# Queries and keys of a dilated attention layer: one wide matmul for both parts of the tokens, and the rotary swap as transfers

## The chip, the core and the metric

The kernel runs on one core of a Trainium2 chip. The metric is the device time of one execution in microseconds (us), the median of three runs. A profile of one more execution comes with it; its rows give the times of single instructions on the engines: TensorE (PE; its weight loads are PEld), VectorE (DVE), ScalarE (ACT), GpSimd (POOL), and SyncE (SP), which issues the loads of weights.

## What is computed

The reference is a trunk of two layers on 256 tokens of width 1024, in float32. The even layer mixes neighbourhood attention and latent attention, the odd layer is the one below, and a squared-ReLU MLP stands behind each.

```python
def odd_mixer(xn, w_in, w_o, cos_f, sin_f):
    hcat = (xn @ w_in).reshape(b, s, DIL_GROUPS, 3, DIL_HEADS, HEAD_DIM)
    q = apply_rope(hcat[:, :, :, 0], cos_f, sin_f)
    k = apply_rope(hcat[:, :, :, 1], cos_f, sin_f)
    v = hcat[:, :, :, 2]
    return dilated_attention(q, k, v) @ w_o

def apply_rope(x, cos, sin):
    x1, x2 = x[..., :half], x[..., half:]
    return jnp.concatenate([x1 * c - x2 * s, x2 * c + x1 * s], axis=-1)
```

There are 3 dilation groups of 16 heads with 64 columns each; `half` is 32. A product with float32 accuracy is made from float32r matmuls: tokens and weights are each split into a high and a low part, and high x high, low x high and high x low are summed.

## The kernel before

Activations lie transposed in SBUF, 8 tiles of 128 features by 256 tokens. `xh` and `xl` are the high and low part of the normed tokens, two tiles from one tag with two buffers. Weights stream in: SyncE loads 1 MB at a time into `raw`, ScalarE casts it to the high part `whi` (L201), VectorE subtracts to the low part `wlo` (L202), each in four pieces; a pool of three buffers holds them.

The function `odd` works in 8 units of two heads in each of three groups. In a unit, `qk_steps` makes three blocks (b = 0, 1, 2) of queries and keys. A block has two halves f of 128 output features and 256 tokens each, and for each half 8 tiles of input features are summed, so 16 calls of `mm3` (L204 to L207), each with three matmuls of 256 columns; both halves lie in one PSUM bank. `rope` (L928) then turns the block: ScalarE copies the four 32-partition quarters, swapped in pairs, from PSUM to the tile `sw` (L931, L932), VectorE multiplies the block by the cosine (L934) and `sw` by the sine (L935) and adds. Block 0 gives queries and keys of the first group (`q0h`, `q0l`), block 1 the queries of the other two (`q12`), block 2 their keys (`k12`, printed `k`, L944). `value_steps` makes the values. `attention` makes the scores of the unit before (L214 from block 0, L967 from `q12` and `k12`), the softmax (L974 to L978), and turned probabilities (L985); `mix` multiplies them with the values of the unit before that (L1000, L1005). `weave` lays these among the matmuls of the next unit.

The order on each engine is set by a scheduler at build time, from the order in which the program is written and its priorities; on the chip each engine takes its instructions in that order. PSUM banks come from two tags, `acc` and `w`, four each. All small temporaries (`sw`, `r1`, `sn`, `pp`) share the tag `scratch` with 12 buffers. GpSimd's queue carries transfers only in the two MLPs (L141, with accumulation).

Of the kernel before, what the change touches and what calls it, by code (L numbers as in the profile page):

```python
# [20 lines left out]
F32R = mybir.dt.float32r  # L21
# [28 lines left out]
def trunk(ctx, tc, a, out):  # L50
# [16 lines left out]

    def half_tile(pool, name, bufs, tag="half"):
        return pool.tile([P, KT, T], F32R, tag=tag, name=name, bufs=bufs)

    def quarter_pair(name):
        return [act.tile([P, KT // 2, T], F32R, tag="quarter", name=name + v, bufs=4) for v in "hl"]
# [119 lines left out]
    def weight():  # L192

        j = state["used"]
        prefetch(j + 1, j + 1)
        prefetch(j + LOAD_AHEAD, j + SPLIT_AHEAD)
        state["used"] = j + 1
        return parts.pop(j)[1:3]
# [38 lines left out]

    def prepare(k, n, xT, ts=slice(0, T)):

        v, hi, lo, gk = x[:, k, ts], xT[0][:, k, ts], xT[1][:, k, ts], gains[:, n * KT + k:n * KT + k + 1]  # L240
        return (lambda: nc.scalar.activation(hi, v, AF.Copy, scale=gk).ins,
                lambda: nc.vector.scalar_tensor_tensor(lo, v, gk, hi.bitcast(F32), ALU.mult, ALU.subtract).ins)  # L242

# [51 lines left out]

    def hand_over(accs, last, n):

        xT = half_tile(act, "xh", 2), half_tile(act, "xl", 2)
        s = sum_tile()
        for b in range(4):  # L300
            last[b]()
            v, acc = x[:, 2 * b:2 * b + 2, :], two(accs[b])
            with tc.high_priority(NORM_PRIO):
                nc.vector.tensor_tensor(v, acc, v, op=ALU.add)
                for f in zip(*(prepare(k, n, xT) for k in (2 * b, 2 * b + 1))):
                    done = [step() for step in f]

        with tc.issue_after(done[0]), tc.issue_after(done[1]):
            state["parts_done"] = [add_squares(b, s) for b in range(4)][-1]
        return xT, s  # L310
# [40 lines left out]
    def mlp(mp, xT, s, apart=(), beside=lambda j, p: None):  # L351

        hs = {}
        quarters = [act.tile([P, KT // 2, T], F32R, tag="quarter", name="hh", bufs=4) for _ in range(3)]

        def up(j, pu):
            w = weight()

            ranges = [range(4), range(4, 6), range(6, 8)] if j == 0 else [range(8)]
            for ks in ranges:
                for f in range(2):
                    for k in ks:
                        c = slice(k * 256 + f * P, k * 256 + f * P + P)
                        mm3(pu[:, (1 - f) * T:(2 - f) * T], w[0][:, c], w[1][:, c], xT[0][:, k, :], xT[1][:, k, :],
                            k == 0 and (f == 0 or j > 0), k == KT - 1 and (f == 1 or j > 0))
            r = scratch([512], "relu")
            nc.scalar.activation(r, pu, AF.Relu)
            h = mp.tile([P, 8, P], F32, tag="h", name="h", bufs=1)  # L370
            nc.scalar.activation(h[:, 4:8, :].rearrange("p (t f) n -> p f t n", f=2), r.rearrange("p (f t n) -> p f t n", f=2, t=2), AF.Square)
            hh = quarters[j % 3].rearrange("p a (b n) -> p (a b) n", n=P)
            hl = mp.tile([P, 7, P], F32R, tag="hl", name="hl", bufs=3)
            hs[j] = hh, hl
            if j < 14:
                nc.vector.tensor_tensor(h[:, 2:4, :], h[:, 7:8, :].broadcast_to([P, 2, P]), h[:, 5:7, :], op=ALU.subtract)
                nc.vector.tensor_tensor(h[:, 1, :], h[:, 5, :], h[:, 3, :], op=ALU.subtract)
                nc.vector.tensor_tensor(h[:, 0, :], h[:, 4, :], h[:, 1, :], op=ALU.subtract)  # L378
                split(hh[:, 0:7, :], hl, h[:, 0:7, :])
            else:  # L380
                split(hh[:, 0:4, :], hl[:, 0:4, :], h[:, 4:8, :])

        def down(j, m):
            wh, wl = weight()
            hh, hl = hs[j]
            first = j == 0
            for n, i, b in SEVEN:
                end = j == 13 and (n not in EIGHT or n in apart)
                mm3(m[n], hh[:, i, :], hl[:, i, :], wh[b], wl[b], first, end)
                if n == "Q3":  # L390
                    beside(j, m["C22"])

        for j in range(3):
            up(j, bank("w"))
        inv = inverse_columns(s)
        m = {n: bank("w" if n in ("P1", "P2", "Q6", "C22") else "acc") for n in ("P1", "P2", "Q6", "C22", "Q7", "Q5", "Q3", "Q4")}
        for j in range(14):
            if j:
                up(j + 2, m["C22"])
            down(j, m)  # L400
        tail = {j: weight() for j in (14, 15)}

        def last(n, o=None, c=slice(0, BLK)):
            o = m[n] if o is None else o
            new = n == "C22" or n in apart
            for j, w in tail.items():
                for i, (at, b) in enumerate(EIGHT[n]):
                    wh, wl = (z[:, b * BLK + c.start:b * BLK + c.stop] for z in w)
                    mm3(o, hs[j][0][:, at, :], hs[j][1][:, at, :], wh, wl, new and (j, i) == (14, 0), (j, i) == (15, 1))

        return m, last, inv
# [9 lines left out]
    def turn_over(m, last, inv, n):  # L421


        xT = half_tile(act, "xh", 2), half_tile(act, "xl", 2)
        s = sum_tile()
        i0, i1 = (column(inv, t) for t in range(NT))
        y = {}

        def turn(t, h, pt):
            with tc.high_priority(NORM_PRIO):  # L430
                for k in range(4):
                    nc.tensor.transpose(pt[:, k * P:(k + 1) * P], y[t, h][:, k * P:(k + 1) * P], ident)
                v = x[:, 4 * h:4 * h + 4, tok(t)]
                nc.vector.tensor_tensor(v, pt.rearrange("p (k n) -> p k n", k=4), v, op=ALU.add)
                for k in range(4 * h, 4 * h + 4):
                    done = [step() for step in prepare(k, n, xT, tok(t))]
            if (t, h) == (1, 0):
                with tc.issue_after(done[0]), tc.issue_after(done[1]):
                    for b in range(4):
                        add_squares(b, s)  # L440

        def step(o, name, scale, v, op=ALU.add):
            with tc.high_priority(NORM_PRIO):
                onto_tokens(o, m[name], scale, v, op)
            return o

        sc = lambda: scratch([512], "y")
        last("P2")
        p0, p1 = sc(), sc()
        nc.scalar.activation(p0, m["P1"], AF.Copy, scale=i0)  # L450
        nc.scalar.activation(p1, m["P1"], AF.Copy, scale=i1)
        y[0, 0] = step(sc(), "P2", i0, p0)
        v0 = step(sc(), "Q6", i0, p0, ALU.subtract)
        v0 = step(v0, "Q5", i0, v0)
        last("Q3")
        turn(0, 0, m["P1"])
        y[0, 1] = step(v0, "Q3", i0, v0)
        v1 = step(sc(), "Q6", i1, p1, ALU.subtract)
        v1 = step(v1, "Q7", i1, v1)
        v2 = step(sc(), "Q5", i1, v1)  # L460
        last("C22")
        turn(0, 1, m["Q6"])
        y[1, 1] = step(v2, "C22", i1, v2)
        last("Q4")
        y[1, 0] = step(v1, "Q4", i1, v1, ALU.subtract)
        return xT, s, [lambda: turn(1, 1, m["P2"]), lambda: turn(1, 0, m["P1"])]
# [81 lines left out]


    def even(ep):  # L550
        xT = xh, xl = half_tile(act, "xh", 2), half_tile(act, "xl", 2)

        def load_x(k, n):
            nc.sync.dma_start(x[:, k:k + n, :], a["x"][:, k:k + n, :])
# [308 lines left out]


    def odd(op, xT, s, late):
        xh, xl = xT
        cosT = op.tile([P, T], F32, name="cosT")
        sinT = op.tile([P, T], F32, name="sinT")
        mask = op.tile([P, NT, 384], F32, name="mask")
# [43 lines left out]
        def qk_steps(d):  # L913
# [3 lines left out]

            def gemm(b, f, half):
                if f == 0 and half == 0:
                    hold["w"], hold["p"] = weight(), bank("acc")  # L920
                (wh, wl), pq = hold["w"], hold["p"]
                for k in range(4 * half, 4 * half + 4):
                    ws = slice((f * KT + k) * P, (f * KT + k + 1) * P)
                    mm3(pq[:, f * T:(f + 1) * T], wh[:, ws], wl[:, ws], xh[:, k, :], xl[:, k, :], k == 0, k == KT - 1)
                if f == 1 and half == 1:
                    rope(b, pq)

            def rope(b, pq):  # L928
                sw, r1 = scratch([512], "sw"), scratch([2, T], "r1")
                for r in range(0, P, 64):  # L930
                    nc.scalar.copy(sw[r:r + 32], pq[r + 32:r + 64])  # L931
                    nc.scalar.copy(sw[r + 32:r + 64], pq[r:r + 32])  # L932
                sw = sw.rearrange("p (f n) -> p f n", f=2)
                nc.vector.tensor_tensor(r1, pq.rearrange("p (f n) -> p f n", f=2), cosT.unsqueeze(1).broadcast_to([P, 2, T]), op=ALU.mult)  # L934
                nc.vector.tensor_tensor(sw, sw, sinT.unsqueeze(1).broadcast_to([P, 2, T]), op=ALU.mult)  # L935
# [201 lines left out]
```

## Time and profile before

| | us |
|---|---|
| median of three runs | 737.83 |
| the runs | 737.17 to 737.85 |
| the profiled execution | 738.17 |
| its span | 736.4 |

The page gives each engine's busy time in the span: TensorE 727.2 us, VectorE 610.5, ScalarE 558.9, GpSimd 79.9. Its slices show the granted clock of TensorE at full speed but for the last. The odd layer lies between about 290 and 545 us. A time at the head of a row is a start, counted from the start of the span; matmuls overlap, so that their pace is read from the distance of two starts and not from their length.

### The profile page before, as it was taken

The page shows a single profiled execution, that of the slowest core. Times are in us where ns is not written, and L with a number is a line of the kernel's source. Part 1 is how long each engine was busy: PE and PEld are TensorE (multiplying, and loading weights), DVE is VectorE, ACT ScalarE, POOL GpSimd, SP SyncE. Part 2 cuts the span into 40 slices and gives each one's busy share as a digit, 9 for nine tenths or more (in the row PEclk, how much of TensorE's full clock was granted, in tenths as well). Part 3 has the DMA queues.
Part 4 walks back from the last instruction along what each step waited for, and adds up shares of the span by engine and source line. Part 5 has one row for each costly group of instructions (what it writes and reads, how often), then busy time and mean ns, then how long its engine had stood idle before and what let it go on. Part 6 is the DMA issues. An engine that isn't in the chain of part 4 may idle for free.

```text
span 736.4 us, 14008 instructions
## 1 busy us (share of the span) xinstructions
PE 727.2 (99%) x5442; PEld 680.7 (92%) x5442; DVE 610.5 (83%) x1090; ACT 558.9 (76%) x1027; POOL 79.9 (11%) x75
## 2 busy tenths in 40 slices
PE   9999999999999999999999999999999999999996
PEld 6988899999999998999999999999999999999995
DVE  6888859999999959887778677776759999999957
ACT  7778968767766756888988989889867768767752
POOL 0100002224212000000000000000003123322000
PEclk9999999999999999999999999999999999999998
DMA  8773338798999643644443444534558699898611
GB/s 312 275 263 131 115 115 216 227 288 236 263 266 261 194 145 150 226 146 140 173 160 144 156 151 171 176 129 160 199 204 216 208 275 262 247 263 249 190 52 57
DMA packets 34178, 143.78 MB, mean 195 GB/s; under 512 B 3776, under 2 KB 5312, under 8 KB 25024
## 3 DMA queue, kind: packets, MB, share of 16 engines
q1 hardware_dynamic: 26208, 127.94, 49.6%
q0 software_dynamic: 7616, 14.68, 12.0%
q8 instruction: 42, 0.69, 0.4%
q10 hardware_dynamic: 288, 0.28, 0.1%
q14 instruction: 24, 0.20, 0.1%
HBM read 141.84 MB, written 1.05 MB: 194 GB/s over the span
## 4 chain that ended last, share of the span: by engine, by line
PE 92%; DVE 4%; ACT 1%; issue 1%; DMA 1%; POOL 0%; SPq 0%; POOLq 0%; DVEq 0%
PE acc L205 17%; PE acc L206 16%; PE acc L207 16%; PE w L205 11%; PE w L206 11%; PE w L207 11%; PE w L214 1%; PE w L985 1%; DVE wlo L202 1%; PE w L801 1%; PE w L967 1%; PE acc L1000 1%; PE w L815 1%; ACT whi L201 1%; DVE xl L242 1%
## 5 line engine op out<-in xcount | busy, mean ns | idle before, releaser
L202 DVE TENSOR_TENSOR wlo<-raw,whi 128x512 fp32r<-128x512 f32 (+3 forms) x360 | 297.0, 846 | 56.0 <-ACT whi L201 55.6
L201 ACT CAST whi<-raw 128x512 fp32r<-128x512 f32 (+3 forms) x360 | 253.8, 745 | 89.4 <-PE w L206 64.8
L206 PE MATMUL w<-xl,whi 128*128 128x256 f32 x528 | 149.6, 283 | 0.1
L207 PE MATMUL w<-xh,wlo 128*128 128x256 f32 x528 | 149.3, 283 | 0.0
L205 PE MATMUL w<-xh,whi 128*128 128x256 f32 x528 | 148.9, 283 | 0.0
L205 PE MATMUL acc<-xh,whi 128*128 128x256 f32 x432 | 125.2, 290 | 0.0
L206 PE MATMUL acc<-xl,whi 128*128 128x256 f32 x432 | 122.3, 283 | 0.0
L207 PE MATMUL acc<-xh,wlo 128*128 128x256 f32 x432 | 122.3, 283 | 0.0
L206 PEld LDWEIGHTS w<-xl,whi 128*128 128x128 f32 x528 | 101.2, 192 | 1.6 <-DVE xl L242 0.6
L205 PEld LDWEIGHTS w<-xh,whi 128*128 128x128 f32 x528 | 101.0, 192 | 1.0
L207 PEld LDWEIGHTS w<-xh,wlo 128*128 128x128 f32 x528 | 101.2, 192 | 0.0
L140 POOL COPY sum<-sum 128x512 f32<-128x512 f32 x28 | 41.4, 1494 | 468.3 <-DVE wlo L202 271.9
L205 PEld LDWEIGHTS acc<-xh,whi 128*128 128x128 f32 x432 | 82.5, 191 | 1.3 <-issue 0.3
L206 PEld LDWEIGHTS acc<-xl,whi 128*128 128x128 f32 x432 | 82.5, 191 | 0.0
L207 PEld LDWEIGHTS acc<-xh,wlo 128*128 128x128 f32 x432 | 82.4, 191 | 0.0
L205 PE MATMUL acc<-whi,xh 128*128 128x384 f32 (+2 forms) x160 | 55.4, 348 | 0.2 <-ACT whi L201 0.2
L206 PE MATMUL acc<-wlo,xh 128*128 128x384 f32 (+2 forms) x160 | 55.1, 344 | 0.4 <-DVE wlo L202 0.4
L207 PE MATMUL acc<-whi,xl 128*128 128x384 f32 (+2 forms) x160 | 54.7, 342 | 0.0
L201 ACT CAST hh<-h 128x896 fp32r<-128x896 f32 (+1 forms) x32 | 28.9, 903 | 18.2 <-DVE h L378 17.2
L205 PE MATMUL w<-whi,hh 128*128 128x512 f32 (+1 forms) x108 | 42.1, 390 | 0.0
L206 PE MATMUL w<-wlo,hh 128*128 128x512 f32 (+1 forms) x108 | 41.5, 384 | 0.0
L207 PE MATMUL w<-whi,hl 128*128 128x512 f32 (+1 forms) x108 | 41.2, 382 | 0.0
(225 smaller groups left out, 1495.4 us busy)
## 6 DMA issues: line engine op xcount, KB each, us to landing
raw<-in_w SPq DMA_DIRECT2D x36, 1024.0 KB, 5.4
raw<-in_w_oqk SPq DMA_DIRECT2D x24, 1024.0 KB, 4.8
raw<-in_w SPq DMA_DIRECT2D x28, 768.0 KB, 5.3
sum<-in_w POOLq DMA_DIRECT2D x28, 512.0 KB, 8.5
raw<-in_w_ov SPq DMA_DIRECT2D x16, 768.0 KB, 4.3
sum<-in_w SPq DMA_DIRECT2D x28, 256.0 KB, 6.1
raw<-in_w_oe SPq DMA_DIRECT2D x4, 1024.0 KB, 6.6
raw<-in_w_oo SPq DMA_DIRECT2D x4, 1024.0 KB, 4.8
```

The source lines that it names most:

```text
L140: nc.gpsimd.tensor_copy(out=sums[:, 1, :], in_=sums[:, 0, :])
L201: a = nc.scalar.copy(hi, src).ins
L202: return a, (eng or nc.vector).tensor_tensor(lo, src, hi.bitcast(F32), op=ALU.subtract).ins
L205: nc.tensor.matmul(o, sh, mh, start=first, stop=False)
L206: nc.tensor.matmul(o, sh, ml, start=False, stop=False)
L207: nc.tensor.matmul(o, sl, mh, start=False, stop=last)
L214: nc.tensor.matmul(o[j], y[pb, 0, ts], z[pb, 1, :], start=n == 0, stop=n == 2)
L242: lambda: nc.vector.scalar_tensor_tensor(lo, v, gk, hi.bitcast(F32), ALU.mult, ALU.subtract).ins)
L801: nc.tensor.transpose(pt[:, b * P:(b + 1) * P], pp[:, b // 2, (b % 2) * P:(b % 2 + 1) * P], ident)
L815: nc.tensor.matmul(pvo[64 * j:64 * j + 64, 0:P], v[:, kk, h * 64:(h + 1) * 64], pts[:, 2 * j + kk, :], start=kk == 0, stop=kk == NT - 1)
L967: nc.tensor.matmul(ss[i, j][rows, T:T + P], d["q12"][:, j, i * P + 64 * c:i * P + 64 * c + 64], d["k12"][:, j, 2 * i + c, :], start=True, ...
L985: nc.tensor.transpose(pt[:, b * P:(b + 1) * P], pp[:, b * P:(b + 1) * P], ident)
```

## The change

The tokens' two parts become one tile `xx` of 2 x 8 x 256 columns (`tokens_pair`), in the place of the two tiles; `xh` and `xl` are views of it. In the odd layer's `qk_steps` one matmul of 512 columns takes both parts of the tokens against the high part of the weight, into the two halves of a bank; the second matmul, low weight by high tokens, adds to the second half. So each half f of a block has a bank of its own. ScalarE copies the second half of the bank to SBUF (`low`), and VectorE adds it to the first, into a scratch tile for the block (`qk`). `rope` reads that tile, and its four swapped quarters are written by four transfers from SBUF to SBUF on GpSimd's queue.

```diff
+    def tokens_pair():
+        return act.tile([P, 2, KT, T], F32R, tag="pair", name="xx", bufs=1)
...
             def gemm(b, f, half):
                 if f == 0 and half == 0:
-                    hold["w"], hold["p"] = weight(), bank("acc")
+                    hold["w"], hold["s"] = weight(), scratch([512], "qk")
+                if half == 0:
+                    hold["p"] = bank("acc")
                 (wh, wl), pq = hold["w"], hold["p"]
                 for k in range(4 * half, 4 * half + 4):
                     ws = slice((f * KT + k) * P, (f * KT + k + 1) * P)
-                    mm3(pq[:, f * T:(f + 1) * T], wh[:, ws], wl[:, ws], xh[:, k, :], xl[:, k, :], k == 0, k == KT - 1)
-                if f == 1 and half == 1:
-                    rope(b, pq)
+                    nc.tensor.matmul(two(pq), wh[:, ws], xT[:, :, k, :], start=k == 0, stop=False)
+                    nc.tensor.matmul(pq[:, T:2 * T], wl[:, ws], xh[:, k, :], start=False, stop=k == KT - 1)
+                if half == 1:
+                    low, o = scratch([T], "low"), hold["s"][:, f * T:(f + 1) * T]
+                    nc.scalar.copy(low, pq[:, T:2 * T])
+                    nc.vector.tensor_tensor(o, pq[:, 0:T], low, op=ALU.add)
+                    if f == 1:
+                        rope(b, hold["s"])
 
             def rope(b, pq):
                 sw, r1 = scratch([512], "sw"), scratch([2, T], "r1")
-                for r in range(0, P, 64):
-                    nc.scalar.copy(sw[r:r + 32], pq[r + 32:r + 64])
-                    nc.scalar.copy(sw[r + 32:r + 64], pq[r:r + 32])
+                for r in (0, 32):
+                    for h in (0, 64):
+                        nc.gpsimd.dma_start(sw[h + r:h + r + 32], pq[h + 32 - r:h + 64 - r])
```

On VectorE, in unit 4 (counted from 0), the turning of the three blocks stands like this before. `r` is a block times the cosine, `q0l` and `q` the results of blocks 0 and 1, `k` that of block 2, `wlo` a split of weights, `pts` turned probabilities.

```order
L934 TENSOR_TENSOR r_5157<-acc,cosT 128x512
L935 TENSOR_TENSOR sw<-sw,sinT 128x512
L202 TENSOR_TENSOR wlo<-raw,whi 128x384
L937 TENSOR_TENSOR r_5157<-r_5157,sw 128x512
...
L934 TENSOR_TENSOR r_5235<-acc,cosT 128x512
L935 TENSOR_TENSOR sw<-sw,sinT 128x512
L202 TENSOR_TENSOR wlo<-raw,whi 128x384
L940 TENSOR_TENSOR q_5013<-r_5235,sw 128x512
...
L934 TENSOR_TENSOR r_5317<-acc,cosT 128x512
L935 TENSOR_TENSOR sw<-sw,sinT 128x512
L202 TENSOR_TENSOR wlo<-raw,whi 128x512
L944 TENSOR_TENSOR k_0_3456<-r_5317,sw 64x8x64 x2
```

And after, in the same unit, with the new additions into `qk`:

```order
L937 TENSOR_TENSOR qk<-acc,low 128x256
L948 TENSOR_TENSOR sw<-sw,sinT 128x512
L937 TENSOR_TENSOR qk<-acc,low 128x256
L950 TENSOR_TENSOR r_5050<-r_5050,sw 128x512
L947 TENSOR_TENSOR r_5120<-qk,cosT 128x512
...
L948 TENSOR_TENSOR sw<-sw,sinT 128x512
L206 TENSOR_TENSOR wlo<-raw,whi 128x512
L953 TENSOR_TENSOR q_4914<-r_5120,sw 128x512
L937 TENSOR_TENSOR qk<-acc,low 128x256
...
L948 TENSOR_TENSOR sw<-sw,sinT 128x512
L206 TENSOR_TENSOR wlo<-raw,whi 128x512
L957 TENSOR_TENSOR k_0_3453<-r_5194,sw 64x8x64 x2
```

The first product with the sine (L948, block 0) now stands ahead of the second addition of block 1, and the product of block 1 ahead of the second addition of block 2. Units 2 and 6 have the same order; in units 3, 5 and 7 the second addition of block 1 stands ahead of block 0's product; in unit 1 the additions of block 2 stand ahead of block 1's product.

On GpSimd, between the odd layer's inverse root and the first transfer of the second MLP, there was nothing:

```order
L265 TENSOR_TENSOR rstd<-ms,mhalf 128x2
L140 COPY sum<-sum 128x512
L141 DMA sum<-in_w 128x2x512
```

Now the 96 transfers stand there:

```order
L269 TENSOR_TENSOR rstd<-ms,mhalf 128x2
L945 DMA sw<-qk 32x512 x96
L144 COPY sum<-sum 128x512
L145 DMA sum<-in_w 128x2x512
```

Four of them belong to each block. On TensorE the matmuls stand in the order of before, but for unit 0, whose scores from `k12` move seven groups of matmuls back.

## Rows read from the trace of the kernel before

**Rows 1.** The page: span, and TensorE's busy time, share and instructions.

```profile
span 736.4 us, 14008 instructions
PE 727.2 (99%) x5442; PEld 680.7 (92%) x5442; DVE 610.5 (83%) x1090; ACT 558.9 (76%) x1027; POOL 79.9 (11%) x75
```

**Rows 2.** Busy time in two stretches of the odd layer; columns as in the first line.

```profile
core 0: us, PE busy (x) PEld busy (x) DVE busy (x) ACT busy (x) POOL busy (x), PEclk, DMA share, GB/s
...
400.00:450.00 50.00, 50.00 (x450) 49.26 (x449) 36.28 (x82) 43.69 (x95) 0.00 (x0) 1.00 0.46 164
450.00:500.00 50.00, 50.00 (x433) 49.32 (x434) 37.61 (x76) 42.77 (x90) 0.00 (x0) 1.00 0.43 148
```

**Rows 3.** Waits of TensorE: waiter, releaser: total us, times, longest.

```profile
PE acc L86 <- DVE warm L81: 1.2, 1, 1.2
PE acc L206 <- DVE wlo L202: 0.4, 2, 0.2
```

**Rows 4.** Timeline of TensorE: start, length, line; runs of 256 and 512 columns.

```profile
349.20 0.28 PE L206 MATMUL acc<-xl,whi 128*128 128x256 f32 x1
...
353.99 0.28 PE L207 MATMUL acc<-xh,wlo 128*128 128x256 f32 x1
...
650.12 0.40 PE L206 MATMUL w<-wlo,hh 128*128 128x512 f32 x1
...
653.32 0.39 PE L205 MATMUL acc<-sumh,hh 128*128 128x512 f32 x1
```

**Rows 5.** Timeline of TensorE, one unit: scores, first block, two transposes, next scores.

```profile
376.97 1.09 PE L967 MATMUL w<-k,q 128*64 128x128 f32 x16
...
379.33 0.39 PE L205 MATMUL acc<-xh,whi 128*128 128x256 f32 x1
...
385.18 0.49 PE L985 MATMUL w<-ident,pp 128*128 128x128 f32 x3
...
389.83 0.49 PE L985 MATMUL w<-ident,pp 128*128 128x128 f32 x3
...
407.32 0.44 PE L967 MATMUL w<-k,q 128*64 128x128 f32 x4
```

**Rows 6.** Timeline of ScalarE and VectorE, third block of that unit.

```profile
396.97 0.58 ACT L931 COPY sw<-acc 32x512 f32<-32x512 f32 x1
...
399.35 0.69 DVE L934 TENSOR_TENSOR r<-acc,cosT 128x512 f32<-128x512 f32 x1 [0.96 <-ACT sw L932]
399.95 0.68 DVE L935 TENSOR_TENSOR sw<-sw,sinT 128x512 f32<-128x512 f32 x1
...
401.15 1.38 DVE L944 TENSOR_TENSOR k<-r,sw 64x512 f32<-64x512 f32 x2
```

**Rows 7.** Groups by line, 345 to 522 us: total busy us, mean ns.

```profile
L931 ACT COPY sw<-acc 32x512 f32<-32x512 f32 x36 | 20.8, 578 | 0.6
L932 ACT COPY sw<-acc 32x512 f32<-32x512 f32 x36 | 20.8, 577 | 0.4
...
L202 DVE TENSOR_TENSOR oal<-acc,oah 128x256 fp32r<-128x256 f32 x4 | 1.7, 424 | 0.1
L201 ACT CAST oah<-acc 128x256 fp32r<-128x256 f32 x4 | 1.5, 373 | 0.1
```

**Rows 8.** Transfers on GpSimd's queue (L141): ns min/median/max, landing; one with its wait.

```profile
L141 POOL DMA_DIRECT2D sum<-in_w x28: 1087/1087/1691, 109.8 to 678.8; - x28
...
DMA to landing us min/median/max: 6.3/8.5/11.3
...
614.83 1.09 POOL L141 DMA_DIRECT2D sum<-in_w  x1 [0.30 <-POOL sum L140]
```

**Rows 9.** Instructions on the tile `sum`: GpSimd's copies, ns min/median/max.

```profile
L140 POOL COPY sum<-sum x28: 607/1183/4820, 108.8 to 676.9; 128x512 f32<-128x512 f32 x28
```

**Rows 10.** Issues of transfers: count, KB each, median us to landing.

```profile
out<-y SPq DMA_DIRECT2D x2, 256.0 KB, 2.0
...
gains<-in_gains ACTq DMA_DIRECT2D x1, 16.0 KB, 2.9
```

More of the change, by code (lines that the diff above doesn't have):

```diff
@@ L238, in prepare @@
     def prepare(k, n, xT, ts=slice(0, T)):
-        v, hi, lo, gk = x[:, k, ts], xT[0][:, k, ts], xT[1][:, k, ts], gains[:, n * KT + k:n * KT + k + 1]
+        v, hi, lo, gk = x[:, k, ts], xT[:, 0, k, ts], xT[:, 1, k, ts], gains[:, n * KT + k:n * KT + k + 1]
         return (lambda: nc.scalar.activation(hi, v, AF.Copy, scale=gk).ins,
@@ L296, in hand_over @@
     def hand_over(accs, last, n):
-        xT = half_tile(act, "xh", 2), half_tile(act, "xl", 2)
+        xT = tokens_pair()
         s = sum_tile()
@@ L365, in up @@
                         c = slice(k * 256 + f * P, k * 256 + f * P + P)
-                        mm3(pu[:, (1 - f) * T:(2 - f) * T], w[0][:, c], w[1][:, c], xT[0][:, k, :], xT[1][:, k, :],
+                        mm3(pu[:, (1 - f) * T:(2 - f) * T], w[0][:, c], w[1][:, c], xT[:, 0, k, :], xT[:, 1, k, :],
                             k == 0 and (f == 0 or j > 0), k == KT - 1 and (f == 1 or j > 0))
@@ L421, in turn_over @@
     def turn_over(m, last, inv, n):
-        xT = half_tile(act, "xh", 2), half_tile(act, "xl", 2)
+        xT = tokens_pair()
         s = sum_tile()
@@ L550, in even @@
     def even(ep):
-        xT = xh, xl = half_tile(act, "xh", 2), half_tile(act, "xl", 2)
+        xT = tokens_pair()
+        xh, xl = (xT[:, i] for i in range(2))
         def load_x(k, n):
@@ L865, in odd @@
     def odd(op, xT, s, late):
-        xh, xl = xT
+        xh, xl = (xT[:, i] for i in range(2))
         cosT = op.tile([P, T], F32, name="cosT")
```

## The prediction

> **What bounds the kernel now.** I read the page first: the span is 736.4 us, and TensorE is busy for 727.2 of it [rows 1]. The table by stretches then says which engine is full in the odd layer, the only place where the change alters work: between 400 and 500 us TensorE is busy in all of both 50 us, at full clock, ScalarE for 43.7 and 42.8, VectorE for 36.3 and 37.6, GpSimd for none [rows 2]. TensorE's own list of waits holds nothing longer than the 1.2 us at the start, and its second entry totals 0.4 us over the whole run [rows 3]. So in the odd layer nothing waits for ScalarE or VectorE: what is taken off TensorE there is gained, what is taken off ScalarE is not, and a new wait of TensorE costs its full length.
>
> **The matmuls: a gain of 4.1 us.** In a run of matmuls of 256 columns the starts go from 349.20 to 353.99 in 40 steps, 0.120 us each; in the MLP, matmuls of 512 columns go from 650.12 to 653.32 in 14 steps, 0.229 us each [rows 4]. A group (one weight tile, both parts) costs 3 x 0.120 = 0.359 us before and 0.229 + 0.120 = 0.348 us after, 0.0108 us less. There are 8 units x 3 blocks x 2 halves x 8 tiles = 384 groups: 4.1 us. The columns are as many as before; what goes is one matmul's fixed part of about 11 ns. The rows of 512 columns read one stretch, the new operand has two stretches of 256, which no row shows. The gain is at most these 4.1 us, and nothing if the second stretch costs what a matmul of its own does; I take 4.1, as the count of columns is the same.
>
> **ScalarE and VectorE: no direct cost.** ScalarE loses 96 copies of 0.58 us (55.6 us) and gains 48 copies of 256 columns, nearest row 0.37 us (17.8 us) [rows 7]. VectorE gains 48 additions; the nearest row is 0.42 us [rows 7], 2.5 us per unit of 30.35 us (376.97 to 407.32 [rows 5]), about 24.9 us busy instead of 22.4. Neither is full, and TensorE covers both. The accumulator banks, nine instead of six uses per unit out of four, come free after a copy and an addition, some 1.5 to 3 us after the last matmul, and are wanted again after three other uses, at least 5.6 us: hidden.
>
> **The swap: from 2.4 us to about 6.** In one unit the chain of today stands in [rows 6]: the first copy of the third block (keys of the second and third group) starts at 396.97, the first product at 399.35, the key tile is done at 401.15 + 1.38 = 402.5. The scores read it at 407.32 [rows 5], 4.8 us later, which is why nobody waits. After the change the swap is four DMAs on GpSimd's queue. They cannot start before VectorE's second addition, and VectorE's product waits for the last of them. I call S the time from that addition to the product. A hand-over to GpSimd takes 0.30 us and an issue 1.09 us [rows 8]; three issues go ahead of the last. No row shows 64 KB from SBUF to SBUF on that queue. The fastest landing of any transfer is 2.0 us (an output of 256 KB late in the program, when little else moves), a small load at the start takes 2.9 [rows 10], and the fastest on GpSimd's queue 6.3 (512 KB with accumulation, beside full engines) [rows 8]. I take 2.4, between the two small ones, since the transfer engines are 0.46 and 0.43 busy in this stretch [rows 2]. S = 0.30 + 3 x 1.09 + 2.4 = 6.0 us; bounds 5.6 and 9.9. If an issue of 32 rows is shorter than these of 256, S falls below 5.6; 0.8 each gives 4.7.
>
> On VectorE the product stands in a strict row, and the next block's addition stands behind it, as the order of unit 4's instructions shows; so one block's transfers hold back the next block's. This is a new serial chain that TensorE can end up waiting for. Its deadline, from TensorE's rows [rows 5]: the first block's second half ends 12 groups after 379.33, at 383.64, and the scores start at 407.32, 23.7 us later; less 36 groups x 0.0108 that is 23.3 us. For the second block (end 389.83) it is 17.3 us.
>
> Units 2, 4 and 6 (counted from 0) have all three swaps in one chain: 2.6 us to the first block's addition (copy 0.4, addition 0.4, three operations of 0.6 ahead of it [rows 6]), S, product 0.6 and addition 0.4, S, product 0.6, on average one other operation, addition 0.4 (1.7 together), S, product 0.6, a split 0.6, key tile 1.4 and a hand-over 0.1: 8.0 + 3S. Against 23.3 the wait is 3S - 15.3 us. Units 3 and 5 have the second block's addition ahead of the first product, so two swaps: 4.5 + 2S against 17.3, a wait from S = 6.4. In unit 0 the scores stand 23 groups (8.0 us) and 12 score matmuls (0.9) behind the third block's end, 20.1 us from the first block's; its chain has 9.9 + 2S, a wait of 2S - 10.2. Unit 1 has no such order, unit 7's scores come later, behind its values and output products: nothing there. With S = 6.0: 3 x 2.7 + 0 + 1.8 = 9.9 us. While TensorE waits, VectorE's later work slips by the same time; I add nothing for that.
>
> [...] The trace shows the issue on GpSimd's queue at 1.09 us as median and minimum [rows 8], while the copy beside it takes from 0.61 to 4.82 us [rows 9]. [...]
>
> **The sum.** The profiled execution took 738.17 us, 1.8 beyond its span; the median is 0.34 lower. 738.17 - 4.1 + 9.9 - 0.34 = 743.6 us.
>
> **Rivals.** The swap stays hidden, and the kernel is faster. It decides at S: the waits of all units are 3 x (3S - 15.3) + 2S - 10.2, zero from S = 5.1 down, and equal to the gain at S = 5.5. For it: the issues in the rows carry eight times as many rows as the new ones, and a transfer of 64 KB is small beside weights of 1 MB. Against it: even the fastest landing and today's issue give 5.6. Full gain: 733.7 us.
>
> They cancel: S between 5.35 and 5.6 gives 736.4 to 739.2, no change. For it: the fastest landing row lies there. Against it: it is a narrow band.
>
> GpSimd is held up: an issue at the maximum row of 1.69 us [rows 8] or a landing behind weights makes S 7 to 7.8. For it: the copies of 4.82 us [rows 9]. [...] S = 7.0 gives 17.1 + 2.4 (units 3 and 5) + 3.8 = 23.3 us of waits, 757.0 us; S = 7.8 about 769.
>
> The wide matmul brings nothing: the second stretch costs a matmul's fixed part. Then 4.1 us more in every case, 747.7 with S = 6.0. For it: no row has such an operand. Against it: the columns bound these matmuls.
>
> **How the numbers follow.** A difference of 0.2%, 1.5 us, is about what a measurement of this kernel can tell from no change. Forecast, S from 5.6 to 7.0: 0.50 (with the matmul rival inside it, 0.05). Hidden swap: 0.28. Cancelling: 0.12. Held up, beyond 757: 0.10. So faster 0.28, same 0.12, slower 0.60. The likeliest case's own range is 739.3 to 757. The range must take in the faster cases, down to 733.6, and leaves out the last case at the top: 733.6 to 757.0.
>
> **What would show it.** Starts of a wide matmul and its narrow one 0.348 us apart as a pair: the gain. GpSimd busy some 105 us more, in fours of 1.09. The product of the swapped tile preceded by a wait on DMA, and the wait of TensorE on that line's key tile, about 2.7 us in units 2, 4 and 6 and none in unit 7: the chain. If TensorE's list of waits stays empty in the odd layer, S is under 5.1 and the forecast is wrong; if the waits sit at accumulators or at weight splits instead, the bank or the row on VectorE was misjudged. If the pair takes 0.359, the first term is wrong.

## The result, and the profile after

The changed kernel took 740.68 us (median of 4 runs, 739.63 to 741.42), the kernel before 737.84 (4 runs, 737.17 to 738.10): a ratio of 1.0038, 95% interval 1.0025 to 1.0050. It is slower by 2.8 us where 5.8 were forecast. The four runs stand in two pairs, 741.42 us twice and 739.63 and 739.95, and the profile is of one of the upper pair, so that its span (739.6 us against 736.4) differs by more than the medians.

The page of the changed kernel, two lines that answer to [rows 1], and behind them the stretch from 400 to 450 us, answering to [rows 2]:

```profile
span 739.6 us, 13461 instructions
PE 726.4 (98%) x5058; PEld 661.4 (89%) x5058; DVE 622.7 (84%) x1130; ACT 518.9 (70%) x987; POOL 125.1 (17%) x171
...
400.00:450.00 50.00, 50.00 (x374) 45.81 (x374) 39.75 (x90) 38.37 (x92) 8.15 (x17) 1.00 0.58 189
```

TensorE is still full in the middle of the odd layer. Its list of waits has one new entry, at the head (waiter, releaser: total us, times, longest; before, [rows 3]):

```profile
PE w L980 <- DVE k L957: 2.5, 1, 2.5
PE acc L90 <- DVE warm L85: 1.2, 1, 1.2
```

L980 is the scores of the second and third group, L957 writes their key tile: the wait that was forecast, on the line that was forecast, but once only and in unit 0. The timeline of TensorE has the scores of units 0 to 2 (answering to the score rows of [rows 5]) and what follows on the wait:

```profile
326.38 1.86 PE L980 MATMUL w<-k,q 128*64 128x128 f32 x16 [2.48 <-DVE k L957]
328.17 0.79 PE L932 MATMUL acc<-xx,whi 128*128 128x512 f32 x1
...
349.90 1.09 PE L980 MATMUL w<-k,q 128*64 128x128 f32 x16
...
379.96 1.09 PE L980 MATMUL w<-k,q 128*64 128x128 f32 x16
```

Before, units 1 and 2 had their scores at 346.62 and 376.97. So the changed kernel is 3.28 us late at unit 1. From then on it wins back: unit 1 to 2 takes 30.06 us instead of 30.35. By the first score of unit 7 it is 1.50 us late (531.93 against 530.43), at the last output's issue 0.96 (733.96 against 733.00). But its span is 3.28 us longer: 2.3 us come behind the last output's issue, where the kernel computes nothing. The row on GpSimd's sequencer shows what stands there (first of before, then of the changed kernel; ns min/median/max, start of the first and last):

```profile
L1131 POOLq DRAIN  x3: 40/93/2975, 731.6 to 736.1; - x3
```

```profile
L1144 POOLq DRAIN  x3: 46/98/6277, 732.6 to 739.4; - x3
```

GpSimd's drain at the end took 2.98 us and ended at 734.6, ahead of the last output's landing (735.46). Now it takes 6.28 us and ends at 738.9, 2.5 us after the last output has landed (736.40), and the program ends when it does.

The swap's transfers, by line (answering to [rows 8]):

```profile
L945 POOL DMA_DIRECT2D sw<-qk x96: 496/496/592, 305.7 to 523.3; - x96
...
DMA to landing us min/median/max: 1.8/2.1/5.0
```

An issue takes 0.50 us and not 1.09; a transfer lands after 1.8 to 5.0 us.

### The profile page after: what moved, and what is told of

It reads as the page before. It is cut to its first block, busy times and chain, and to the rows that moved or that the text cites. A ratio compares the mean times of both kernels' runs of the same rounds, so it can differ in the third digit from the quotient of the medians.

```text
span 739.6 us, 13461 instructions
## 1 busy us (share of the span) xinstructions
PE 726.4 (98%) x5058; PEld 661.4 (89%) x5058; DVE 622.7 (84%) x1130; ACT 518.9 (70%) x987; POOL 125.1 (17%) x171
## 4 chain that ended last, share of the span: by engine, by line
PE 94%; DVE 2%; issue 1%; DMA 1%; ACT 1%; POOL 0%; SPq 0%; POOLq 0%; ACTq 0%; DVEq 0%
PE w L209 12%; PE w L210 12%; PE w L211 12%; PE acc L932 12%; PE acc L209 11%; PE acc L210 11%; PE acc L211 11%; PE acc L933 6%; PE w L218 1%; PE w L998 1%; PE w L980 1%; PE w L806 1%; PE acc L1013 1%; PE w L820 1%; DMA raw<-in_w_cv 1%
## 5 line engine op out<-in xcount | busy, mean ns | idle before, releaser
L210 PE MATMUL w<-xx,whi 128*128 128x256 f32 x528 | 149.6, 283 | 0.0
L211 PE MATMUL w<-xx,wlo 128*128 128x256 f32 x528 | 149.3, 283 | 0.0
L209 PE MATMUL w<-xx,whi 128*128 128x256 f32 x528 | 148.9, 283 | 0.0
L932 PE MATMUL acc<-xx,whi 128*128 128x512 f32 x384 | 139.8, 405 | 0.0
L933 PE MATMUL acc<-xx,wlo 128*128 128x256 f32 x384 | 108.2, 282 | 0.0
L210 PEld LDWEIGHTS w<-xx,whi 128*128 128x128 f32 x528 | 101.2, 192 | 1.4 <-DVE xx L246 0.2
L209 PEld LDWEIGHTS w<-xx,whi 128*128 128x128 f32 x528 | 101.0, 192 | 1.0
L211 PEld LDWEIGHTS w<-xx,wlo 128*128 128x128 f32 x528 | 101.2, 192 | 0.0
L932 PEld LDWEIGHTS acc<-xx,whi 128*128 128x128 f32 x384 | 72.5, 189 | 16.7 <-issue 0.3
L933 PEld LDWEIGHTS acc<-xx,wlo 128*128 128x128 f32 x384 | 73.0, 190 | 0.0
L209 PE MATMUL acc<-whi,xx 128*128 128x384 f32 (+2 forms) x160 | 55.8, 351 | 0.0
L210 PE MATMUL acc<-wlo,xx 128*128 128x384 f32 (+2 forms) x160 | 55.4, 346 | 0.2 <-DVE wlo L206 0.2
L211 PE MATMUL acc<-whi,xx 128*128 128x384 f32 (+2 forms) x160 | 54.7, 342 | 0.0
```

The costliest lines, as they stand in the source:

```text
L209: nc.tensor.matmul(o, sh, mh, start=first, stop=False)
L210: nc.tensor.matmul(o, sh, ml, start=False, stop=False)
L211: nc.tensor.matmul(o, sl, mh, start=False, stop=last)
L932: nc.tensor.matmul(two(pq), wh[:, ws], xT[:, :, k, :], start=k == 0, stop=False)
L933: nc.tensor.matmul(pq[:, T:2 * T], wl[:, ws], xh[:, k, :], start=False, stop=k == KT - 1)
```

## The experiments

Eleven kernels ran, with five rounds each where not said otherwise; the kernel before gave 737.6 to 737.8 us beside them. The first theory, A, was that the whole loss is unit 0's: the wait of 2.48 us and a slow clock behind it (granted 0.50 for 3.41 us), which the author put at 1.8 us. Without both, the time would be 740.7 - 4.3 = 736.4 us, 735.5 to 737.3.

**Unit 0 by ScalarE.** `tiles` holds unit 0's tiles; `pq` is the block's sum in SBUF.

```diff
+                if d is tiles[0]:
+                    for r in range(0, P, 64):
+                        nc.scalar.copy(sw[r:r + 32], pq[r + 32:r + 64])
+                        nc.scalar.copy(sw[r + 32:r + 64], pq[r:r + 32])
+                else:
                     for r in (0, 32):
...
```

> Unit 0 alone swaps by four ScalarE copies from SBUF again; units 1 to 7 keep the transfers. [...] Theory B (the transfers cost something in every unit, by contention or on VectorE's row): at most 1 us is won, 739.5 or more.

Measured: 737.96 us (11 runs), 1.0005 of before (0.9996 to 1.0014). 2.7 us are won and not 4.3. TensorE's wait is 1.3 us instead of 2.5 (with unit 0's scores back where they stood before the change, seven groups of matmuls earlier), and its clock stays at 1.00 behind it; but the end is nearly as long as in the changed kernel, with 84 of the 96 transfers left:

```profile
PE w L985 <- DVE k L962: 1.3, 1, 1.3
```

```profile
L1150 POOLq DRAIN  x3: 46/93/5747, 728.8 to 735.1; - x3
```

So unit 0 is a part of the loss, and theory A falls as the only cause. The last row led to the drain.

**All swaps by ScalarE.**

```diff
-                for r in (0, 32):
-                    for h in (0, 64):
-                        nc.gpsimd.dma_start(sw[h + r:h + r + 32], pq[h + 32 - r:h + 64 - r])
+                for r in range(0, P, 64):
+                    nc.scalar.copy(sw[r:r + 32], pq[r + 32:r + 64])
+                    nc.scalar.copy(sw[r + 32:r + 64], pq[r:r + 32])
```

> All swaps by ScalarE copies from SBUF, so that only the wide matmul and the additions are left of the change. Theory A: as with unit 0 alone, 736.4 us, if ScalarE keeps up; it has 21.8 of 30 us busy per unit with transfers, and 12 copies of 0.58 make it 28.7 of 30. Theory C (ScalarE is full then): TensorE waits for weight splits or copies in every unit, 738.5 us or more.

Measured: 744.91 us, 1.0095 (1.0082 to 1.0109). Theory C: ScalarE is busy for 44.99 of 50 us, and TensorE waits for its probabilities (L991) ahead of the transposes; from unit 3 to unit 6 each takes 31.3 to 31.5 us instead of 30.05. The rows are the stretch from 400 to 450 us (columns as in [rows 2]) and the first wait of TensorE:

```profile
400.00:450.00 50.00, 47.80 (x359) 43.06 (x358) 38.63 (x87) 44.99 (x101) 0.00 (x0) 1.00 0.41 141
```

```profile
PE w L998 <- ACT pp L991: 5.0, 5, 1.3
```

**One stretch of 512 columns.**

```diff
-        return act.tile([P, 2, KT, T], F32R, tag="pair", name="xx", bufs=1)
+        return act.tile([P, KT, 2, T], F32R, tag="pair", name="xx", bufs=1).rearrange("p k v n -> p v k n")
```

> The two parts of the tokens lie side by side for each weight tile, so that the wide matmul reads one stretch of 512 columns instead of two of 256; all else as in the changed kernel. Theory D (the pair of matmuls takes 0.353 us in most of the odd layer instead of 0.348 because of the second stretch): 0.347 everywhere, about 320 groups x 0.006 = 1.9 us less, 738.8 us. Theory E (the step is not of the operand): pairs at 0.353 as before, 740.7 us, within 1 us.

Measured: 740.48 us, 1.0037 (1.0024 to 1.0049): theory E. A unit takes 30.05 us again, and its pairs settle at 0.353 us again. One row is worth more than the verdict. TensorE waited 2.32 us in unit 0 here too, but the granted clock behind the wait stayed full, where it had fallen to 0.50 in the changed kernel. The stretch from 326 to 330 us, of the changed kernel and of this one:

```profile
326.00:330.00 4.00, 3.62 (x21) 3.08 (x22) 3.79 (x12) 2.16 (x6) 0.00 (x0) 0.57 0.29 111
```

```profile
326.00:330.00 4.00, 3.30 (x29) 2.90 (x30) 3.94 (x12) 1.99 (x6) 0.00 (x0) 1.00 0.40 148
```

From unit 0's scores to unit 1's it is 23.52 us in the one and 21.90 in the other: the fall costs 1.6 us, when it comes. The length of the wait alone doesn't decide it: one of 2.28 us, in a kernel further down, brought it as well (23.52 us to unit 1's scores again), and one of 2.32 didn't. Why, these rows don't tell.

**The swap alone**, in the kernel before.

```diff
-                for r in range(0, P, 64):
-                    nc.scalar.copy(sw[r:r + 32], pq[r + 32:r + 64])
-                    nc.scalar.copy(sw[r + 32:r + 64], pq[r:r + 32])
+                qk = scratch([512], "qk")
+                nc.scalar.copy(qk, pq)
+                for r in (0, 32):
+                    for h in (0, 64):
+                        nc.gpsimd.dma_start(sw[h + r:h + r + 32], qk[h + 32 - r:h + 64 - r])
```

> The kernel before with its three matmuls of 256 columns, where one ScalarE copy of 128x512 to SBUF and the four transfers take the place of the four ScalarE copies. Theory A (swap in unit 0 is all that costs): TensorE waits in unit 0 and its clock falls, as in the changed kernel, 737.8 + 4.3 = 742.1 us, between 740 and 744; no wait in the later units. Theory F (the additions and their place in VectorE's row made the wait, not the transfers): no wait, 737.8 us.

Measured: 744.27 us (742.08 to 746.08), 1.0090 (1.0074 to 1.0106), just above theory A's 744, which did not know of the drain. One wait, in unit 0, of 3.65 us with a fall of the clock behind it (granted 0.57 from 329 to 333 us), and a drain of 6.28 us; nothing in the later units:

```profile
PE w L969 <- DVE k L946: 3.6, 1, 3.6
```

So theory F falls: the additions aren't needed for the wait; the transfers, with the copy to SBUF ahead of them, bring it.

**More transfers, nothing else.** TensorE, VectorE, ScalarE and SyncE keep the order of the kernel before, instruction by instruction.

```diff
+        junk = op.tile([P, 512], F32, name="junkd")
...
+                for r in range(0, P, 32):
+                    nc.gpsimd.dma_start(junk[r:r + 32, 0:32], cosT[r:r + 32, 0:32])
```

> The kernel before, its work and its order unchanged on TensorE, VectorE, ScalarE and SyncE, with 96 transfers of 4 KB from one constant to a tile that nobody reads, on GpSimd's queue in the odd layer. Theory G (GpSimd's drain at the end grows with the transfers that its queue has issued, 2.98 us with 28 and 6.28 with 124, and ends after the outputs have landed): drain 6.3 us, 5.7 instead of 3.4 us from the last output's issue to the end, 737.8 + 2.3 = 740.1 us. Theory H (the long end belongs to the swap itself): 737.8 us, drain 3.0.

Measured: 740.22 us (740.02 to 740.28), 1.0031 (1.0020 to 1.0043): theory G. Nobody waits for these transfers, TensorE waits nowhere for longer than before, the last output is issued at 732.7 us, and the kernel is 2.5 us slower.

```profile
L1134 POOLq DRAIN  x3: 46/98/6279, 731.3 to 738.1; - x3
```

Over the kernels, the drain is 2.98 us with 28 transfers on GpSimd's queue, 5.75 with 112, 6.28 with 124 and 8.77 with 220: about 0.03 us for each. It goes by transfers and not by rows: the 28 have 256 rows each, more rows together than the 96 new ones of 32.

**A drain ahead of the end**, in the code ahead of the next-to-last instruction of GpSimd.

```diff
+        nc.gpsimd.drain()
         r = rsqrt(ss[:, 2:3], "x")
```

> The changed kernel with one drain of GpSimd in the last MLP, ahead of its next-to-last instruction, where it waits over 40 us for VectorE. Theory G1 (a drain pays for the transfers since the last drain): the final drain is under 3 us, 740.7 - 2.3 = 738.4 us. Theory G2 (each drain pays for all transfers of the program, or none but the last is long): 740.7 us or more.

Measured: 741.04 us, 1.0042 (1.0028 to 1.0056). The experiment failed: the drain waits for nothing, and was set to the start of the program (0.98 us), ahead of all transfers. Whether a drain in mid-program takes the cost with it stays open. As a repeat of the changed kernel it shows the same wait in unit 0 (2.28 us), the same fall of the clock (granted 0.993 in the mean of the span in both) and the same long end.

**Copies by GpSimd.**

```diff
-                for r in (0, 32):
-                    for h in (0, 64):
-                        nc.gpsimd.dma_start(sw[h + r:h + r + 32], pq[h + 32 - r:h + 64 - r])
+                for r in range(0, P, 64):
+                    nc.gpsimd.tensor_copy(sw[r:r + 32], pq[r + 32:r + 64])
+                    nc.gpsimd.tensor_copy(sw[r + 32:r + 64], pq[r:r + 32])
```

> The changed kernel with the swap as four GpSimd copies of 32x512 instead of four transfers. No transfers, so the drain is 3.0 us and no landing behind weights. Theory A+G (unit 0's wait by transfers landing behind weights, its clock, and the drain are all of the loss): S = 0.3 + 4 x 0.6 to 1.2 = 2.7 to 5.1 us, 740.7 - 2.3 - 2.5 to 4.3 = 734.1 to 735.9 us. Theory I (GpSimd's copies are slowed by VectorE to 2 us or more, as the copy of 4.82 us shows can be): S over 8, waits of TensorE in units 2, 4 and 6, 745 us or more.

Measured: 772.17 us, 1.0465 (1.0451 to 1.0479): slower, as theory I said, and far over its price, but not by its cause: a copy took under 1 us and the median S is 3.76 us, less than with the transfers. TensorE's longest waits are for VectorE's weight splits (10.6 us in 10 waits) and, in unit 0, for the key tile (5.4 us), and its clock is lowered for 27.3 us in five places (granted 0.978 in the mean of the span, 0.993 in the changed kernel). VectorE waits 15.1 us for the copies, in all 24 of its products with the sine. By line, the copy and the product with the cosine, which has 0.68 us in the changed kernel:

```profile
L945 POOL COPY sw<-qk x48: 608/975/980, 306.3 to 556.4; 32x512 f32<-32x512 f32 x48
```

```profile
L947 DVE TENSOR_TENSOR r<-qk,cosT x24: 682/1097/1101, 305.7 to 553.7; 128x512 f32<-128x512 f32 x24
```

Beside the copies VectorE's product takes 1.10 us; the product with the sine, of the same shape, waits for the last copy and takes 0.69. (The row has 48 of the 96 copies.)

**The transfers on ScalarE's queue.**

```diff
-                        nc.gpsimd.dma_start(sw[h + r:h + r + 32], pq[h + 32 - r:h + 64 - r])
+                        nc.scalar.dma_start(sw[h + r:h + r + 32], pq[h + 32 - r:h + 64 - r])
```

> The changed kernel with the 96 transfers on ScalarE's queue instead of GpSimd's. Theory A+G: the drain falls back to 3.0 us, unit 0 still waits for transfers that land behind weights: 740.7 - 2.3 = 738.4 us, 736.5 to 739.5. Theory J (ScalarE stands still while a transfer waits for VectorE's addition, and its copies and weight casts come late): waits of TensorE for weights or copies in later units, 742 us or more.

Measured: 735.93 us (735.47 to 736.08), 0.9972 (0.9961 to 0.9982): faster than both kernels, and under the range of theory A+G. The drain is 2.97 us, and the wait of unit 0 went too, down to 0.5 us. That isn't because the transfers landed sooner: the last of unit 0's first swap landed 5.1 us after its issue here too. But the scheduler, given another queue, also put VectorE's row in another order. The second addition of block 1 now stands ahead of block 0's product, where it stood behind it in the changed kernel, so that this addition no longer waits for the first swap:

```profile
309.93 0.42 DVE L937 TENSOR_TENSOR qk<-acc,low 128x256 f32<-128x256 f32 x1
312.68 0.69 DVE L948 TENSOR_TENSOR sw<-sw,sinT 128x512 f32<-128x512 f32 x1 [2.33 <-DMA sw<-qk]
```

How much of the gain is the queue's and how much the order's was not separated, but for the drain.

**Without the swap.**

```diff
-                for r in (0, 32):
-                    for h in (0, 64):
-                        nc.gpsimd.dma_start(sw[h + r:h + r + 32], pq[h + 32 - r:h + 64 - r])
...
-                nc.vector.tensor_tensor(sw, sw, sinT.unsqueeze(1).broadcast_to([P, 2, T]), op=ALU.mult)
+                nc.vector.tensor_tensor(sw, pq.rearrange("p (f n) -> p f n", f=2), sinT.unsqueeze(1).broadcast_to([P, 2, T]), op=ALU.mult)
```

> The changed kernel without the swap: its transfers are left out, and VectorE's sine product reads the unswapped tile (this part of the rotary embedding is not computed). What is left is the wide matmul with its copies and additions. Theory K (gain as the trace's pairs show it, 0.347 us in unit 0 and 0.353 behind it, against 0.359 before): 80 x 0.012 + 304 x 0.0065 = 2.9 us less than before, 734.9 us, 734.3 to 735.6. Prediction's first term: 4.1 us less, 733.7 us. If the additions or their place cost something by themselves, 736 us or more.

Measured: 735.69 us (735.23 to 736.59), 0.9974 (0.9963 to 0.9985). The wide matmul with its copies and additions is worth 1.9 us. Theory K's 2.9 is nearer than the prediction's 4.1, but the medians give 1.0 us less. In the profiled execution the last output is issued 3.8 us earlier than before, of which the landing of that output gives 0.9 back (3.35 us instead of 2.46); so the spans differ by 2.9 us, as theory K has it. Why the medians don't isn't explained.

**A slower swap** (one round): eight transfers of 256 columns per block.

```diff
-                        nc.gpsimd.dma_start(sw[h + r:h + r + 32], pq[h + 32 - r:h + 64 - r])
+                        for c in (0, 256):
+                            nc.gpsimd.dma_start(sw[h + r:h + r + 32, c:c + 256], pq[h + 32 - r:h + 64 - r, c:c + 256])
```

> The changed kernel with eight transfers of 256 columns per block instead of four of 512: four more issues of 0.49 us, so S is 2.0 us longer. Theory L (the prediction's chain on VectorE, which the changed kernel just escaped: the key tile is done 0.06 to 0.38 us ahead of the scores in units 2, 4 and 6): waits of 3 x 2.0 - 0.3 = 5.7 us in units 2, 4 and 6, about 1 us in 3 and 5, 4 more in unit 0, a drain 3.3 us longer, and up to 1.7 us of slow clock behind each long wait: 765 to 777 us. Theory M (blocks don't chain; only one S counts per unit): 2 us in units 2, 4, 6 and 0 and the drain, 750 to 754 us.

Measured: 768.91 us, 1.0423 (1.0404 to 1.0442), inside theory L and beyond M. Two us more for one swap cost 28 us. But not by the two us alone: VectorE's order changed too, and in units 3, 5 and 7 the second addition of block 1 now stands behind block 0's product, where it stood ahead of it. And the pieces aren't quite L's: the waits for the key tile stand in units 0 and 2 to 6 with 3.1, 2.1, 2.0, 4.7, 1.1 and 1.5 us, and other TensorE waits (weight splits, values), the drain of 8.77 us and 17 us of slow clock in four places (granted 0.983 in the mean of the span) stand beside them.

```profile
PE w L981 <- DVE k L958: 14.4, 6, 4.7
PE acc L210 <- DVE wlo L206: 3.0, 6, 1.2
PE acc L209 <- ACT v L914: 2.0, 1, 2.0
```

**The transfers on SyncE's queue.**

```diff
-                        nc.gpsimd.dma_start(sw[h + r:h + r + 32], pq[h + 32 - r:h + 64 - r])
+                        nc.sync.dma_start(sw[h + r:h + r + 32], pq[h + 32 - r:h + 64 - r])
```

> The changed kernel with the transfers on SyncE's queue, in one row with the loads of the weights. Theory A+G (what counts is who issues and what the drain costs): no long drain, ScalarE not held, 735 to 736.5 us. Theory N (a load of weights that stands behind a transfer waits for VectorE's addition with it, and comes late): TensorE waits for weight splits in every unit, 739 us or more.

Measured: 735.51 us (735.10 to 735.82), 0.9970 (0.9958 to 0.9981), the fastest of all, and level with the kernel that has no swap. The loads of the weights come in time: TensorE waits 0.5 us in unit 0 and not again. The transfers between 302 and 325 us (issues, KB each, median us to landing), of the changed kernel and of this one:

```profile
raw<-in_w_ov SPq DMA_DIRECT2D x2, 768.0 KB, 4.7
...
sw<-qk POOLq DMA_DIRECT2D x16, 64.0 KB, 3.5
```

```profile
raw<-in_w_ov SPq DMA_DIRECT2D x2, 768.0 KB, 4.7
sw<-qk SPq DMA_DIRECT2D x16, 64.0 KB, 2.0
```

In SyncE's row from 300 to 330 us a load of weights is issued ahead of a swap or behind it and never between its transfers, and the swap lands in 2.0 us where it took 3.5; that the row is the reason is argued, not shown. As on ScalarE's queue, VectorE has the second addition of block 1 ahead of block 0's product in unit 0 here, which takes one landing out of the wait's chain by itself. The key tile is done 1.25 us or more ahead of the scores in units 1 to 7, where the changed kernel came down to 0.06.

## Why the prediction was right and wrong

**The bound** was right. No engine but TensorE matters in the odd layer as long as nobody makes it wait, and what was taken off ScalarE was worth nothing (the whole change without the swap wins 1.9 us by the medians).

**The matmuls: mis-sized, 4.1 us forecast, 1.9 to 2.9 measured** (medians and profiles of the kernel without the swap). The prediction took 0.348 us for a pair. It is that in unit 0, and 0.353 in most groups behind it. Starts of the wide matmul in both places, the first and the last of 42 and of 14 pairs (answering to [rows 4]):

```profile
302.13 0.39 PE L932 MATMUL acc<-xx,whi 128*128 128x512 f32 x1
...
316.69 0.39 PE L932 MATMUL acc<-xx,whi 128*128 128x512 f32 x1
...
412.83 0.39 PE L932 MATMUL acc<-xx,whi 128*128 128x512 f32 x1
...
417.78 0.40 PE L932 MATMUL acc<-xx,whi 128*128 128x512 f32 x1
```

14.56 / 42 = 0.347 and 4.95 / 14 = 0.354, against 0.359 before. A unit gains 0.30 us (30.35 to 30.05) and not 0.52. The rival "the wide matmul brings nothing" went in this direction, but its cause, the second stretch of the operand, is not it: with one stretch it is the same. The short spacing comes back in single places (four groups ahead of the scores in each unit); what sets it is open.

**ScalarE and VectorE: right.** The addition takes 0.419 us (0.42 taken), the copy 0.366 (0.37), and with no swap nothing waits for either.

**The swap: the step that failed. The chain is there, but S was too long, by the issue.** The sum was 0.30 for the hand-over, 3 x 1.09 for issues and 2.4 for the last landing. The hand-over is 0.30 us (305.42 to 305.72 in unit 0), and the last landing has a median of 2.37 us over the 24 swaps. The issue is the term that failed: 0.496 us for 32 rows, under half of that for 256 rows in [rows 8]. The prediction named this way out, with 0.8 us an issue and S = 4.7, and took the row that was there instead. From the addition to the last landing the 24 swaps took 3.65 to 6.87 us, median 4.25; from the addition to the product, where VectorE often comes later than the landing, the median is 5.09. By the prediction's own formula S = 0.30 + 3 x 0.50 + 2.4 = 4.2 us gives no wait in any unit: this is its rival of the hidden swap, and in seven of the eight units that rival came true. The margin is thin all the same, since VectorE's other work fills what the issues gave back: in unit 2 the key tile (started at 378.52, two instructions of 1.38 us together) is done at 379.90, and the scores start at 379.96, 0.06 us later. It is 0.38 us in units 4 and 6, where it was 4.8 before.

```profile
378.52 1.38 DVE L957 TENSOR_TENSOR k<-r,sw 64x512 f32<-64x512 f32 x2
```

So the 3 x 2.7 us forecast for these units are zero. The slower swap shows how near the edge was: in these units, where the block's additions and products follow each other as in the changed kernel, TensorE waited 2.1, 4.7 and 1.5 us. In 12 of the 24 swaps the last transfer lands 1.9 to 2.0 us after its issue, in the other 12 after 2.8 to 5.0 us.

**Unit 0: forecast 1.8 us, measured 2.5 and up to 1.6 more.** Here the first swap's S was 6.95 us, since the last transfer of the first swap landed 5.0 us after its issue. VectorE stood still for it, with the next addition behind:

```profile
312.37 0.69 DVE L948 TENSOR_TENSOR sw<-sw,sinT 128x512 f32<-128x512 f32 x1 [1.81 <-DMA sw<-qk]
312.98 0.42 DVE L937 TENSOR_TENSOR qk<-acc,low 128x256 f32<-128x256 f32 x1
```

That transfer was issued at 307.31 us; a load of 768 KB of weights had been issued at 307.28 and landed at 312.08, the transfer at 312.29. The third swap of the unit goes the same way: issued from 318.56 us, beside weights that land at 322.81, it lands at 323.02 to 323.56, with S = 5.37. The prediction had this as a rival ("a landing behind weights"), for all units. It does come in later units too (in unit 3 a transfer issued at 400.66 lands at 404.50, behind weights that land at 404.33), but there it cost TensorE nothing. In unit 0 the prediction's 2S - 10.2, with 6.95 + 5.37 in the place of 2S, gives 2.1 us, near the 2.48: the chain was right here, and its S was long by the landing and not by the issue. The packets show what moved meanwhile: from 308.6 to 310.5 us, with the transfer issued, the load's queue (q1) moves 97 packets, and GpSimd's queue (q0) has no row (packets, MB, share):

```profile
q1 hardware_dynamic: 97, 0.60, 81.1%
```

After that, from 310.5 to 312.08 us, GpSimd's queue moves 32 packets, beside 64 of the load's queue. How the two queues share the transfer engines, no run shows.

**The clock: not in the prediction.** It priced a wait at its length. Behind unit 0's wait TensorE's granted clock was 0.50 for 3.41 us in the profiled execution (0.57 in the mean from 326 to 330 us), which costs 1.6 us by the comparison with the kernel that waited nearly as long (2.32 us) and kept its clock.

**The end: a term at nothing in the prediction, 2.3 us measured.** It counted GpSimd's 96 transfers by their S alone. No row of before says that the drain grows. But the trace of before had what the question needs: a drain of 2.98 us on the engine that is given 96 more instructions, which ended 0.9 us ahead of the last landing.

**The sum.** Forecast: -4.1 + 9.9 = 5.8 us against the profiled execution, or as much against the median. Measured, by kernels that stand for the parts: -2.1 (all but GpSimd's queue: SyncE's queue, 735.51 against 737.63, with its other order on VectorE), +2.5 (96 transfers on GpSimd's queue that nobody waits for), and what is left to +2.8 is 2.4, unit 0's wait and clock. In the profile of unit 0 it is 2.48 less the 0.45 us that are left on SyncE's queue, so 2.0, and 1.6 more where the clock falls; 2.4 lies between. So the wait that was forecast came in one unit of eight, and that the sign came out right was luck: without the 2.5 us of GpSimd's end, which the prediction had not seen, the changed kernel would be at about 738.2 us, level with before (an estimate from these differences).

**What would have shown it** came out mixed: the product waits for DMA in 9 of the 24 swaps, the scores' line waits for the key tile in unit 0 only, GpSimd is 45 us more busy and not 105, in fours of 0.50 us.

## What to carry to other kernels

An engine that is idle is not a free place for transfers: look at what stands at its end, and count the transfers that its queue will have issued (here 96 more made GpSimd's drain 3.3 us longer). When the next owner of a small transfer stands in a strict row, try the queues of the other engines, that of the weight loads too; here SyncE's queue turned a loss of 2.8 us into a gain of 2.1, and ScalarE's into one of 1.8, in part by the shorter end and in part, not separated, by landings and by VectorE's new order. Compare the orders before a difference is put down to the queue. And a chain that crosses engines several times is worth a margin in microseconds and not only a wait of zero: two microseconds more per swap, with the order that came with them, turned no wait into waits in five more units.

## What the runs showed of the hardware that was not expected

- GpSimd's drain at the end took 2.98, 5.75, 6.28 and 8.77 us with 28, 112, 124 and 220 transfers issued from its queue, alike for 96 more of 4 KB and of 64 KB (6.28 us both), and the program waits for it: with 96 more that nobody reads it took 2.5 us longer.
- A transfer of 64 KB issued beside a load of weights on another queue landed 0.2 us behind the load, 5.0 us after its issue instead of 1.9; not every transfer beside a load did (in unit 3 one of block 1 landed after 1.98 us).
- An issue on GpSimd's queue took 0.50 us for 32 rows of 2 KB, and 0.51 us and more on SyncE's and ScalarE's queues (medians 0.58 and 0.60).
- A pair of a wide and a narrow matmul has two settled spacings, 0.347 and 0.353 us, with the same instructions, and stays in one of them until other matmuls come between.
- VectorE's product of two SBUF operands took 1.10 us beside GpSimd's copies from SBUF to SBUF and 0.68 beside the transfers, whose issues took 0.496 to 0.592 us there.
